# Second feed-forward block of a diffusion layer: up product as seven products of block sums, gated features kept in DRAM

## The chip, the cores and the metric

The kernel runs on one core of one Trainium2 chip. The metric is the device time of one execution in microseconds (us). The kernel before was run three times; the profile is of one further execution of it.

## What is computed

One layer over 1024 latent tokens and 256 context tokens, all float32, model width 1024, hidden width 2816. The change lies in the second SwiGLU block and in the steps around it, cut here from the reference:

```python
def layer_norm(x, g, b):
    mu = jnp.mean(xf, axis=-1, keepdims=True)
    var = jnp.mean(jnp.square(xf - mu), axis=-1, keepdims=True)
    return ((xf - mu) * lax.rsqrt(var + LN_EPS)).astype(x.dtype) * g + b

def post_norm(stream, update, g, b):
    return layer_norm(DN_ALPHA * stream + update, g, b)

def modulate(h, shift, scale):
    return h * (1 + scale) + shift

def swiglu(h, w_up, w_down):
    a, g = jnp.split(h @ w_up, 2, axis=-1)
    return (jax.nn.silu(g) * a) @ w_down

# in the layer: first SwiGLU block, then the mixer (attention and state space), then
x = post_norm(x, mod[5] * y, ln_g[layer, 1], ln_b[layer, 1])      # y: output projection of the mixer
x = post_norm(x, 0.5 * mod[8] * swiglu(modulate(x, mod[6], mod[7]), ffn2_w_up[layer], ffn2_w_down[layer]),
              ln_g[layer, 2], ln_b[layer, 2])
```

The context tokens do not reach this last part: it works on the 1024 latent tokens alone.

## The kernel before

Every large product is made of three TensorE products. An operand is split into a rounded part and the rest (`split`: ScalarE writes the rounded part, L132, VectorE the rest, L133), and `mm3` (L234) adds high by high, high by low and low by high into one PSUM bank.

**Weights** are one stream of units of 512 KB in the order of their use (`plan`). `w_dma` loads a unit into one of three buffers `ws`; `w_split` splits half a unit (128 x 512) into one of four pairs `wh`, `wl`; `take` hands out the next half units and splits up to four half units ahead. All transfers of the kernel, weights or not, are issued by one queue, SyncE's (`dq` is `nc.sync`), in the order in which the program writes them. Each engine works through its own list in that order too; a waiting instruction holds up all behind it on its engine.

**Output projection.** `token_major(8, 4, ...)` makes 512 tokens at a time: for each half of the output columns (`hf`) it goes through the eight contraction tiles and four tiles of 128 tokens. `tails=(2, 2)`: the last two contraction tiles go token tile by token tile, so that the results leave one after the other. `evac` (L1374, L1375) scales a result and adds the residual on VectorE; `norm` takes statistics by halves. Its `rest` normalises the tiles later, as a generator that `pump` moves on by a step after each unit of weights.

**Second block.** Two rounds `b` over 512 tokens each; in each, `ffn` makes two halves `h` of the hidden width. `ffn_up` makes 11 hidden tiles: `by_feature` for the linear half (one unit, 8 contraction tiles x 3 products of 128 x 512), again for the gate, then `gate` (L263 to L266: SiLU on ScalarE, product on VectorE, split of the result into `HA`, `HB`). `token_major(11, 4, ...)` follows with the down product, out of these same buffers. The up weights are loaded and split once for each `b`. The input of the second round is transposed and split by `transposed` beside the down product of the first round. The very last tiles have `TAIL = 8` contraction tiles token tile by token tile, and `out_now` (L1427, L1428) finishes and stores each at once.

## Time and profile before

| | |
|---|---|
| time of three runs | 2245.5, 2247.68, 2248.1 us (median 2247.68) |
| span of the profiled execution | 2243.0 us |
| the time outside the span, by the median | 4.7 us |
| TensorE busy in the span | 2200.6 us (98%) |
| VectorE, ScalarE, GpSimd busy | 1466.8, 735.6, 22.3 us |
| granted TensorE clock, mean | 0.998 |
| transfers | 336.67 MB, mean 150 GB/s |

The span runs from the first to the last instruction of the profiled execution; the runs' times hold the start and end of the program as well, so the sum is made on the span and carried over with the 4.7 us. Busy TensorE is not TensorE at its peak, since its matmuls overlap: what counts is the distance from one matmul's start to the next one's.

### The profile page before, as it was taken

Reading aid. Unit: us, or ns where it says so; the run is one execution under the profiler, and the core shown is the slowest. Engines: PE = TensorE matmul, PEld = TensorE weight load, DVE = VectorE, ACT = ScalarE, POOL = GpSimd, SP = SyncE. Lnnn points to the kernel's source line nnn. Section 1 sums busy time; section 2 is a strip of 40 time slices with the busy share of each in tenths; the row PEclk is TensorE's granted clock in tenths of the full one; section 3 lists DMA queues with packets and bytes.
Section 4 is the critical chain, followed back from the end, with each engine's and each line's share of the span. In section 5 each row is a group of like instructions: output and inputs, shape, how many; then the busy total and the mean of one; then the engine's idle time right before and its main releaser. Section 6 shows DMA issues by size and latency. Waiting matters only on the chain.

```text
span 2243.0 us, 32802 instructions
## 1 busy us (share of the span) xinstructions
PE 2200.6 (98%) x12536; PEld 1978.9 (88%) x12536; DVE 1466.8 (65%) x3257; ACT 735.6 (33%) x1575; POOL 22.3 (1%) x33
## 2 busy tenths in 40 slices
PE   7999999999999999999999899999999999999998
PEld 6998999889998999899899799888888888888886
DVE  7788878797888786554777467885334367334336
ACT  4322223423322223333222577433322332332331
POOL 0000000000000000000000000000000000000000
PEclk9999999999999999999999999999999999999999
DMA  9787713436433345235776763332222223322222
GB/s 348 251 294 252 264 67 114 157 125 205 133 126 123 113 133 186 84 113 193 254 262 217 189 154 95 141 131 94 97 101 94 95 93 127 108 96 102 94 94 84
DMA packets 153964, 336.67 MB, mean 150 GB/s; under 512 B 17352, under 2 KB 84936, under 8 KB 153808
## 3 DMA queue, kind: packets, MB, share of 16 engines
q1 hardware_dynamic: 153808, 334.59, 44.6%
q8 instruction: 98, 1.61, 0.3%
q14 instruction: 58, 0.48, 0.1%
HBM read 285.80 MB, written 54.70 MB: 152 GB/s over the span
## 4 chain that ended last, share of the span: by engine, by line
PE 89%; DMA 4%; DVE 3%; ACT 2%; issue 1%; SPq 1%; POOL 0%; POOLq 0%; DVEq 0%; ACTq 0%
PE pb L236 18%; PE pb L237 18%; PE pb L235 18%; PE pb L295 9%; PE pb L297 9%; PE pb L296 9%; PE pb L1251 2%; PE pb L1071 1%; PE pb L1226 1%; DMA bd<-ub 1%; PE pb L348 1%; DMA ws<-wu 1%; DVE row L231 1%; PE pb L1200 1%; ACT z L1211 1%
## 5 line engine op out<-in xcount | busy, mean ns | idle before, releaser
L235 PE MATMUL pb<-X,wh 128*128 128x384 f32 (+2 forms) x2272 | 762.9, 336 | 0.0
L237 PE MATMUL pb<-X,wl 128*128 128x384 f32 (+2 forms) x2272 | 760.6, 335 | 0.0
L133 DVE TENSOR_TENSOR wl<-ws,wh 128x512 fp32r<-128x512 f32 x596 | 395.7, 687 | 305.7 <-ACT wh L132 304.1
L132 ACT ACTIVATE wh<-ws 128x512 fp32r<-128x512 f32 x596 | 357.7, 625 | 597.3 <-PE pb L297 356.6
L236 PE MATMUL pb<-X,wh 128*128 128x512 f32 (+2 forms) x1408 | 486.2, 345 | 0.0
L235 PEld LDWEIGHTS pb<-X,wh 128*128 128x128 f32 x2272 | 429.6, 189 | 28.9
L237 PEld LDWEIGHTS pb<-X,wl 128*128 128x128 f32 x2272 | 429.3, 189 | 28.7 <-DVE wl L133 0.2
L295 PE MATMUL pb<-wh,HA 128*128 128x512 f32 x840 | 329.2, 392 | 2.2 <-DVE hid L264 1.7
L296 PE MATMUL pb<-wl,HA 128*128 128x512 f32 x840 | 326.9, 389 | 0.0
L236 PEld LDWEIGHTS pb<-X,wh 128*128 128x128 f32 x1408 | 265.7, 189 | 25.2
L236 PE MATMUL pb<-XT,wh 128*128 128x256 f32 (+2 forms) x864 | 274.4, 318 | 0.4 <-DVE XT L133 0.4
L264 DVE TENSOR_TENSOR hid<-pb,hid 128x384 f32<-128x384 f32 (+2 forms) x132 | 73.2, 555 | 237.6 <-ACT hid L263 237.4
L295 PEld LDWEIGHTS pb<-wh,HA 128*128 128x128 f32 x840 | 157.8, 188 | 35.7 <-DVE hid L264 2.6
L296 PEld LDWEIGHTS pb<-wl,HA 128*128 128x128 f32 x840 | 157.8, 188 | 31.9
L263 ACT ACTIVATE hid<-pb 128x384 f32<-128x384 f32 (+2 forms) x132 | 64.6, 489 | 359.4 <-PE pb L237 359.4
L236 PEld LDWEIGHTS pb<-XT,wh 128*128 128x128 f32 x864 | 163.8, 190 | 4.6 <-DVE XT L133 0.8
L297 PE MATMUL pb<-wh,HA 128*128 128x512 f32 x416 | 162.0, 389 | 0.0
L297 PE MATMUL pb<-wh,HB 128*128 128x512 f32 x408 | 158.8, 389 | 0.0
L265 ACT ACTIVATE HA<-hid 128x384 fp32r<-128x384 f32 (+2 forms) x132 | 69.3, 525 | 142.5 <-DVE hid L264 142.5
L297 PEld LDWEIGHTS pb<-wh,HA 128*128 128x128 f32 x416 | 78.1, 188 | 16.5
L297 PEld LDWEIGHTS pb<-wh,HB 128*128 128x128 f32 x408 | 76.6, 188 | 16.0
L1251 PE MATMUL pb<-XE,row 128*128 128x64 f32 x512 | 64.6, 272 | 0.0
(355 smaller groups left out, 2616.2 us busy)
## 6 DMA issues: line engine op xcount, KB each, us to landing
ws<-wu SPq DMA_DIRECT2D x184, 512.0 KB
ws<-wd SPq DMA_DIRECT2D x88, 512.0 KB
XE<-wada SPq DMA_DIRECT2D x36, 512.0 KB
HX<-wada SPq DMA_DIRECT2D x36, 512.0 KB
XE<-s5m SPq DMA_DIRECT2D x21, 768.0 KB
HX<-s5m SPq DMA_DIRECT2D x11, 768.0 KB
HA<-wada SPq DMA_DIRECT2D x16, 512.0 KB
ws<-wo SPq DMA_DIRECT2D x16, 512.0 KB
```

Of the source, the lines that this page charges most:

```text
L132: S.activation(h, src, AF.Copy)
L133: V.tensor_tensor(l, src, h.bitcast(F32), op=ALU.subtract)
L235: mm(p, lhsT=wh, rhs=xh, start=first, stop=False)
L236: mm(p, lhsT=wh, rhs=xl, start=False, stop=False)
L237: mm(p, lhsT=wl, rhs=xh, start=False, stop=last)
L263: S.activation(t, g, AF.Silu)
L264: V.tensor_tensor(t, a, t, op=ALU.mult)
L265: S.activation(h, t, AF.Copy)
L295: mm(b[t], lhsT=h, rhs=wh, start=f + i == 0, stop=False)
L296: mm(b[t], lhsT=h, rhs=wl, start=False, stop=False)
L297: mm(b[t], lhsT=l, rhs=wh, start=False, stop=f + i == nf - 1)
L1251: mm(o, lhsT=p, rhs=v, start=m == 0, stop=m == len(ks) - 1)
```

## The change

The second block's up product treats all 1024 tokens at once. Its weights of a hidden tile, the contraction (1024) and the tokens (1024) are each taken in two halves, the linear and the gate part of a tile as the two halves of the third side. In place of the eight products of 4 contraction tiles that this takes, seven are made, between sums of the blocks (the scheme of Strassen in Winograd's form):

- `seven(ua)` gives the seven left operands of a hidden tile: three halves of units as they are, and four sums `s1` to `s4` that VectorE makes in a tile `row` ahead of the split. The order of the products is in `ORDER`.
- `RB[1..7]` are the seven right operands, each four tiles of 128 x 512 with their two parts, made once. Those of products 1 and 2 hold the first 512 tokens (`left_part`, beside the output projection, which also writes them to DRAM as `xf`). The other five are made by `right1` to `right5`, which `ramp` calls after the second to the seventh product; they read `xf` back and transpose the second 512 tokens there.
- `product` makes one product in one bank; `add` puts the seven results together on VectorE; `gated` multiplies, splits and stores the gated tile in DRAM (`hd`, 1 MB a tile).
- The down product of all 22 hidden tiles follows, twice 512 tokens: `hid_load` reads the 22 tiles back before the first round, and `follow` those of the second round in the second half of the first.
- The normalised rows of the output projection go to DRAM (`xh2`) and come back as `z2` after the up product. The second 512 rows are normalised at once (`normed`), and the output projection's last pass has a tail of four contraction tiles. The last norm is made at once by `out_now` in both rounds.
- Five buffers for up units (three `ws`, two in `HX`), weight order and layout of the down weights adapted; the first block and the mixer run as before.

```diff
+    def seven(ua):
+        ug = ua + 1
+        h = lambda u, j: wst[u][:, j * 512:(j + 1) * 512]
+        def s1():
+            r = sums_of[ua] = rowt()
+            V.tensor_tensor(r[:, 0:512], h(ug, 0), h(ug, 1), op=ALU.add)
+            return r[:, 0:512]
...
+        return {1: ((ua,), lambda: h(ua, 0)), 2: ((ua,), lambda: h(ua, 1)), 3: ((ua,), s4), 4: ((ug,), lambda: h(ug, 1)),
+                5: ((ug,), s1), 6: ((ua,), s2), 7: ((ua, ug), s3)}
+    ORDER = [(0, 1), (0, 2), (1, 1), (1, 2), (0, 5), (1, 5), (0, 6), (1, 6), (0, 7), (1, 7), (0, 4), (0, 3), (1, 4), (1, 3)]
+    ORDER += [(f, i) for f in range(2, NF) for i in (1, 5, 6, 2, 7, 4, 3)]
...
+    def w_next(margin):
+        u = pos[0]
+        if u >= len(units) or (margin and u >= barred[0]):
+            return False
+        b = home[u][0] if u in home else turn_w[0] % NWS
+        if b in owner and last_use[owner[b]] >= pos[1] - margin:
+            assert margin, (u, b)
+            return False
+        if u in home:
+            w = home[u][1]
+        else:
+            turn_w[0] += 1
+            w = wp.tile([128, 1024], F32, name=nm("ws"), tag="ws", bufs=NWS)
+        owner[b] = u
+        nc.sync.dma_start(w, units[u])
+        wst[u] = w
+        pos[0] += 1
+        return True
...
+    def left_part(zs):
+        for k0 in (4, 6, 0, 2):
+            ks = (k0, k0 + 1)
+            bs, xs = [bank("T") for _ in ks], [half("hid") for _ in ks]
+            for k, b in zip(ks, bs):
+                for t, x in enumerate(zs):
+                    nc.tensor.transpose(b[:, t * 128:(t + 1) * 128], x[:, k * 128:(k + 1) * 128], ident)
+            V.tensor_scalar(xs[0], bs[0], gB[:, 0, k0:k0 + 1], gB[:, 1, k0:k0 + 1], op0=ALU.mult, op1=ALU.add)
+            S.activation(xs[1], bs[1], AF.Identity, scale=gB[:, 0, k0 + 1:k0 + 2], bias=gB[:, 1, k0 + 1:k0 + 2])
+            for k, x in zip(ks, xs):
...
+    def normed(t, mv, rs):
+        z = zz[4 + t]
+        V.tensor_scalar(z, z, mv[:, 0:1], rs, op0=ALU.subtract, op1=ALU.mult)
+        dq.dma_start(xh2[4 + t], z)
...
+        token_major(8, 4, src, evac, 2.2, (2, 4) if b else (2, 2), kinds="me" if b else "wm",
+                    beside=() if b else last_steps())
...
+    for i in range(2):
+        dq.dma_start(ht[:, i * 1024:(i + 1) * 1024], xf[i])
+        dq.dma_start(me[:, i * 1024:(i + 1) * 1024], xf[2 + i])
...
+    def right1(ks):
+        bs = [turned_z(k) for k in ks]
+        for k, b in zip(ks, bs):
+            V.scalar_tensor_tensor(t1f[k], b, gB[:, 0, k:k + 1], x11[k], op0=ALU.mult, op1=ALU.subtract)
+        for k in ks:
+            split(RB[5][0][k], RB[5][1][k], t1f[k])
+    def right2(ks):
+        bs, xs = [turned_z(k + 4) for k in ks], [half("hid") for k in ks]
+        for k, b, x in zip(ks, bs, xs):
+            S.activation(x, b, AF.Identity, scale=gB[:, 0, k + 4:k + 5], bias=gB[:, 1, k + 4:k + 5])
+            V.tensor_tensor(t1f[k], x, t1f[k], op=ALU.subtract)
+        for k, x in zip(ks, xs):
+            split(RB[6][0][k], RB[6][1][k], t1f[k])
+            split(RB[3][0][k], RB[3][1][k], x)
+    def right3(k):
+        V.scalar_tensor_tensor(x11[k], x11[k], gB[:, 1, k:k + 1], t1f[k], op0=ALU.add, op1=ALU.subtract)
+        split(RB[7][0][k], RB[7][1][k], x11[k])
...
+    def gated(f):
+        s = st2.pop(f)
+        zA, zB = s["A"], s["B"]
+        V.tensor_tensor(zA, zA, zB, op=ALU.mult)
+        o = hring[f % 2]
+        S.activation(o[:, 0:1024].bitcast(F32R), zA, AF.Copy)
+        yield
+        V.tensor_tensor(o[:, 1024:2048].bitcast(F32R), zA, o[:, 0:1024], op=ALU.subtract)
+        yield
+        dq.dma_start(hd[f], o)
...
+    def product(f, i):
+        settle()
+        w = take()[0]
+        s = st2.setdefault(f, {})
+        take_bank(s, i)
+        prod(s[i][0], w, RB[i])
+        if i == 1:
+            s["A"] = ztile()
+            S.activation(s["A"][:, 0:512], s[1][0], AF.Copy)
+            bfree.append(s.pop(1)[1])
+        if i == 7:
+            s["B"] = ztile()
+        A, B = s.get("A"), s.get("B")
+        lo, hi_ = slice(0, 512), slice(512, 1024)
+        if i == 6:
+            add(A[:, hi_], s, 6, A[:, lo])
+            s["u2"] = True
+        if i in (2, 6) and 2 in s and "u2" in s:
+            add(A[:, lo], s, 2, A[:, lo])
+        if i == 7:
+            add(B[:, hi_], s, 7, A[:, hi_])
+            add(A[:, hi_], s, 5, A[:, hi_], False)
+        if i == 4:
+            add(B[:, lo], s, 4, B[:, hi_])
+            add(B[:, hi_], s, 5, B[:, hi_])
+            S.activation(B, B, AF.Silu)
+        if i == 3:
+            add(A[:, hi_], s, 3, A[:, hi_])
+            later2.append(gated(f))
...
+    def ramp(n):
+        if n in (2, 3):
+            right1(range(2 * n - 4, 2 * n - 2))
+        elif n in (4, 5):
+            right2(range(2 * n - 8, 2 * n - 6))
+            if n == 5:
...
+    def hid_load(b, f):
+        if f < len(hid_room):
+            t = hid_room[f]
+            hid2[f] = t.rearrange("p (i t) -> p i t", i=2)
+            dq.dma_start(hid2[f].bitcast(F32), hd[f].rearrange("p (i t) -> p i t", i=2)[:, :, b * 512:(b + 1) * 512])
...
+    for f, i in ORDER:
+        product(f, i)
+        nprod += 1
+        ramp(nprod)
...
+    for j in range(4, NF):
+        hid_load(0, j)
+    hx = slott("HX", [128, NHX])
+    fin = [hx[:, 0:1024], hx[:, 1024:2048]]
+    z2 = [ztile() for _ in range(4)]
+    for t in range(4):
+        dq.dma_start(z2[t], xh2[t])
+    for n, i in (("g1", 2), ("b1", 3)):
+        rows[n] = rowt()
+        row_load(rows[n], i)
...
+        half_done, rest = norm(out_now)
...
+        def follow():
+            for _ in range(NF - 2):
+                yield
+            for f in range(NF):
+                if f:
+                    hid_load(1, f - 1)
+                yield
+        fol = follow()
+        token_major(NF, 4, src, evac, 2.0, (2, TAIL) if b else (2, 2), "dd", () if b else fol)
```

How the lists stand at three places. **First**, VectorE behind the output projection's second 512 tokens (`st`, `mv`, `rs` are the statistics of a tile, `XE` and `z` its rows, `wl` the rest of a weight half, `hid` the gate). Before, the normalisations (L334) of three of the four tiles:

```order
L322 BN_AGGR mv_15383<-st_15152 128x2
L324 TENSOR_SCALAR rs_15385<-mv_15383 128x1
L334 TENSOR_SCALAR XE_10579<-XE_10579,mv_15368,rs_15370 128x1024
L133 TENSOR_TENSOR wl_15390<-ws_15289,wh_15389 128x512
L133 TENSOR_TENSOR wl_15394<-ws_15289,wh_15393 128x512
L334 TENSOR_SCALAR XE_10579<-XE_10579,mv_15373,rs_15375 128x1024
L264 TENSOR_TENSOR hid_15425<-pb_15343,hid_15425 128x512
L133 TENSOR_TENSOR wl_15430<-ws_15341,wh_15429 128x512
L133 TENSOR_TENSOR wl_15434<-ws_15341,wh_15433 128x512
L334 TENSOR_SCALAR z_14781<-z_14781,mv_15378,rs_15380 128x1024
```

Now, the end of the last token tile (L1494 normalises it), then the first splits and sums of the second block (L166 is `s1`, L1550 `right1`, which reads `HB`, the block that came back from DRAM):

```order
L401 BN_STATS st_15183<-z_14806 128x6
L408 BN_AGGR mv_15382<-st_15183 128x2
L410 TENSOR_SCALAR rs_15384<-mv_15382 128x1
L1494 TENSOR_SCALAR z_14806<-z_14806,mv_15382,rs_15384 128x1024
L134 TENSOR_TENSOR wl_15401<-ws_15263,wh_15400 128x512
L134 TENSOR_TENSOR wl_15405<-ws_15263,wh_15404 128x512
L166 TENSOR_TENSOR row_15425<-HX_15206 128x512
L134 TENSOR_TENSOR wl_15424<-row_15425,wh_15423 128x512
L1550 SCALAR_TENSOR_TENSOR HB_15389<-pb_15442,gB,HB_15389 128x512
L1550 SCALAR_TENSOR_TENSOR HB_15389<-pb_15447,gB,HB_15389 128x512
L134 TENSOR_TENSOR HA_15395<-HB_15389,HA_15395 128x512 x2
L166 TENSOR_TENSOR row_15460<-ws_15265 128x512
```

The normalisations stood spread out between the next units' splits; each now stands ahead of all of these, directly behind its tile's statistics, and the making of the right operands stands between the splits.

**Second**, SyncE's queue where the down product begins. Before, from the up weights (`wu`) of a half to its down weights (`wd`):

```order
L149 DMA ws_18599<-wu 128x1024
L149 DMA ws_18638<-wu 128x1024
L149 DMA ws_18674<-wd 128x1024
L149 DMA ws_18713<-wd 128x1024
L149 DMA ws_18749<-wd 128x1024
```

Now, from the last of 18 loads of gated tiles (`hd`, 512 KB each; four more and the first three units `wd` stand further ahead, the store of the last gated tile directly ahead of the 18) to the fourth and fifth unit of down weights:

```order
L1681 DMA XT_18654<-hd_14540 128x2x512
L1708 DMA z_18675<-xh_107 128x1024
L1708 DMA z_18676<-xh_107 128x1024
L1708 DMA z_18677<-xh_107 128x1024
L1708 DMA z_18678<-xh_107 128x1024
L455 DMA row_18683<-lnr 128x1024
L455 DMA row_18685<-lnr 128x1024
L455 DMA HX_18674<-lnr 128x1024 x2
L218 DMA ws_18699<-wd 128x1024
L218 DMA ws_18737<-wd 128x1024
```

VectorE at the same place (L1595, L1599: the last gated tile; L1722, L1724: the rows `z` that came back from DRAM times and plus the rows that came with them):

```order
L1595 TENSOR_TENSOR z_18512<-z_18512,z_18592 128x1024
L1599 TENSOR_TENSOR XE_15643<-z_18512,XE_15643 128x1024
L134 TENSOR_TENSOR wl_18696<-ws_18599,wh_18695 128x512
L1722 TENSOR_TENSOR z_18675<-z_18675,row_18683 128x1024
L1724 TENSOR_TENSOR z_18675<-z_18675,row_18685 128x1024
L134 TENSOR_TENSOR wl_18716<-ws_18601,wh_18715 128x512
L1722 TENSOR_TENSOR z_18676<-z_18676,row_18683 128x1024
```

The fourth unit now stands behind 26 other transfers, and the split of the fifth half unit (`wl_18716`) behind two steps that need four of the last of them.

**Third**, VectorE between the two rounds of the down product. Before (L334, L1406, L1407: norm of the first round, beside the second round's up product):

```order
L322 BN_AGGR mv_17970<-st_17705 128x2
L324 TENSOR_SCALAR rs_17972<-mv_17970 128x1
L334 TENSOR_SCALAR XE_10579<-XE_10579,mv_17955,rs_17957 128x1024
L1406 TENSOR_TENSOR XE_10579<-XE_10579,A_2157_15327 128x1024
L1407 TENSOR_TENSOR XE_10579<-XE_10579,A_2158_15328 128x1024
L133 TENSOR_TENSOR wl_17980<-ws_17880,wh_17979 128x512
L133 TENSOR_TENSOR wl_17984<-ws_17880,wh_17983 128x512
L334 TENSOR_SCALAR HX_14046<-HX_14046,mv_17960,rs_17962 128x1024
```

Now the last of the four tiles, L1739 and L1740 its norm, then the splits of the second round's third half unit and on:

```order
L1751 TENSOR_TENSOR pb_19104<-pb_19104,row_18637 128x512
L1752 SCALAR_TENSOR_TENSOR z_18678<-z_18678,pb_19104 128x512
L401 BN_STATS st_19100<-z_18678 128x6
L408 BN_AGGR mv_19538<-st_19100 128x2
L410 TENSOR_SCALAR rs_19540<-mv_19538 128x1
L1739 SCALAR_TENSOR_TENSOR z_18678<-z_18678,mv_19538,HX_18674 128x1024
L1740 SCALAR_TENSOR_TENSOR z_18678<-z_18678,rs_19540,HX_18674 128x1024
L134 TENSOR_TENSOR wl_19554<-ws_19440,wh_19553 128x512
L134 TENSOR_TENSOR wl_19558<-ws_19440,wh_19557 128x512
```

All four tiles' chains now stand in one piece ahead of the next round's splits, of which two (the first two half units) stand ahead of the chains.

## Rows read from the trace of the kernel before

**Rows 1.** Page, part 1: busy us (share of the span) and instructions.

```profile
PE 2200.6 (98%) x12536; PEld 1978.9 (88%) x12536; DVE 1466.8 (65%) x3257; ACT 735.6 (33%) x1575; POOL 22.3 (1%) x33
```

**Rows 2.** Windows: length; busy PE, PEld, DVE, ACT, POOL; granted clock, DMA share, GB/s.

```profile
1560.00:1580.00 20.00, 20.00 (x90) 16.58 (x89) 10.36 (x15) 6.12 (x11) 0.00 (x0) 1.00 0.30 106
```

**Rows 3.** Timeline, TensorE, up product: start, us, line, instruction.

```profile
1543.44 1.03 PE L362 MATMUL pb<-ident,modl 128*128 128x128 f32 x8
...
1555.22 0.39 PE L235 MATMUL pb<-X,wh 128*128 128x512 f32 x1
...
1560.66 0.39 PE L235 MATMUL pb<-X,wh 128*128 128x512 f32 x1
```

**Rows 4.** Timeline, VectorE, output projection and up product.

```profile
1438.21 0.69 DVE L1374 TENSOR_TENSOR pb<-pb,row 128x512 f32<-128x512 f32 x1
1438.93 0.69 DVE L1375 SCALAR_TENSOR_TENSOR XE<-XE,pb 128x512 f32<-128x512 f32 x1
1439.54 0.69 DVE L1374 TENSOR_TENSOR pb<-pb,row 128x512 f32<-128x512 f32 x1
...
1448.96 1.23 DVE L1294 TENSOR_TENSOR XE<-XE,A 128x1024 f32<-128x1024 f32 x1
1450.11 0.68 DVE L133 TENSOR_TENSOR wl<-ws,wh 128x512 fp32r<-128x512 f32 x1
...
1566.93 0.69 DVE L264 TENSOR_TENSOR hid<-pb,hid 128x512 f32<-128x512 f32 x1 [2.47 <-ACT hid L263]
1568.84 1.29 DVE L133 TENSOR_TENSOR wl<-ws,wh 128x512 fp32r<-128x512 f32 x2 [1.22 <-ACT wh L132]
```

**Rows 5.** Timeline, ScalarE, the same stretch of the up product.

```profile
1567.66 0.63 ACT L265 ACTIVATE HA<-hid 128x512 fp32r<-128x512 f32 x1 [0.76 <-DVE hid L264]
1568.20 1.66 ACT L132 ACTIVATE wh<-ws 128x512 fp32r<-128x512 f32 x3
```

**Rows 6.** Groups by line and shape, ScalarE: count, busy us, mean ns, idle before.

```profile
L132 ACT ACTIVATE X<-A 128x1024 fp32r<-128x1024 f32 x4 | 4.0, 1073 | 0.0
```

**Rows 7.** Waits of the whole span: us in total, times, longest.

```profile
DVE wl L133 <- ACT wh L132: 304.1, 235, 3.3
```

**Rows 8.** Timeline, VectorE, the last four token tiles.

```profile
2217.30 0.70 DVE L508 TENSOR_TENSOR pb<-pb,row 128x512 f32<-128x512 f32 x1 [3.66 <-PE pb L297]
...
2222.74 0.70 DVE L508 TENSOR_TENSOR pb<-pb,row 128x512 f32<-128x512 f32 x1
...
2238.74 0.75 DVE L1428 SCALAR_TENSOR_TENSOR z<-z,rs,A 128x512 f32<-128x512 f32 x1
```

**Rows 9.** Timeline, GpSimd, the power of the variance for the first and last of them.

```profile
2220.03 1.46 POOL L325 TENSOR_TENSOR rs<-rs,mhalf 128x1 f32<-128x1 f32 x1 [336.87 <-DVE rs L324]
...
2236.34 0.92 POOL L325 TENSOR_TENSOR rs<-rs,mhalf 128x1 f32<-128x1 f32 x1 [3.99 <-DVE rs L324]
```

**Rows 10.** Timeline, TensorE, its last matmul.

```profile
2233.19 0.39 PE L297 MATMUL pb<-X,HB 128*128 128x512 f32 x1
```

**Rows 11.** Windows with the transfer engines full (columns as in rows 2).

```profile
28.00:32.00 4.00, 4.00 (x28) 4.00 (x28) 3.96 (x6) 2.25 (x4) 0.00 (x0) 1.00 1.02 403
...
500.00:520.00 20.00, 20.00 (x146) 19.67 (x145) 16.62 (x42) 7.03 (x15) 0.00 (x0) 1.00 1.02 347
```

**Rows 12.** Timeline, SyncE's queue: two loads of 512 KB.

```profile
2205.74 1.53 SPq L149 DMA_DIRECT2D ws<-wd  x2
```

**Rows 13.** Timeline, ScalarE, the split that waited for them.

```profile
2210.43 2.41 ACT L132 ACTIVATE X<-ws 128x512 fp32r<-128x512 f32 x4 [4.69 <-DMA ws<-wd]
```

**Rows 14.** Timeline, TensorE, where attention begins: a wait for transfers.

```profile
1265.21 0.36 PE L1200 MATMUL pb<-HB,HX 128*128 128x256 f32 x1 [2.90 <-DMA HB<-kd]
1266.78 0.45 PE L1201 MATMUL pb<-HA,HX 128*128 128x256 f32 x1 [1.22 <-DMA HA<-kd]
...
1268.31 0.63 PE L236 MATMUL pb<-X,wh 128*128 128x512 f32 x1
1268.74 0.63 PE L237 MATMUL pb<-X,wl 128*128 128x512 f32 x1
```

**Rows 15.** Windows of 2 us at that place (columns as in rows 2).

```profile
1268.00:1270.00 2.00, 2.00 (x6) 1.54 (x6) 0.03 (x1) 0.00 (x0) 0.00 (x0) 0.50 1.02 408
1270.00:1272.00 2.00, 2.00 (x10) 1.65 (x8) 1.38 (x5) 0.00 (x0) 0.00 (x0) 0.92 1.04 423
```

More of the change, by code (lines that the diff above doesn't have):

```diff
@@ L154, in w_split, with item @@
[L154 to L159 removed]
+    units, items, last_use = [], [], {}
+    wst, wsp, apart, sums_of = {}, {}, {}, {}
+    pos, ahead, out_ = [0, 0, 0], [4], [0]
+    home, owner, turn_w = {}, {}, [0]
+    barred = [10 ** 9]
+    def item(us, f):
+        for u in us:
+            last_use[u] = len(items)
+        items.append((max(us), f))
@@ new lines, in w_dma, with w_split @@
+    def w_dma(n):
+        while pos[0] < min(n, len(units)):
+            assert w_next(0)
+    ringed = set()
+    def w_split(n, must):
+        while pos[1] < min(n, len(items)):
+            i = pos[1]
+            if i not in apart and len(ringed) >= 4:
+                assert i >= must, i
+                break
+            u, f = items[i]
+            if u >= barred[0] and i >= must:
+                break
+            w_dma(u + 1)
+            if i in apart:
+                wh, wl = apart.pop(i)
@@ L170, in take @@
         pos[2] += n
-        w_split(i + max(n, ahead[0]))
-        w_dma((i + ahead[0]) // 2 + NWS - 1)
+        for j in list(ringed):
+            if j < i:
+                ringed.discard(j)
+        w_split(i + max(n, ahead[0]), i + n)
+        while w_next(2):
+            pass
         return [wsp.pop(j) for j in range(i, i + n)]
@@ L429, in hybrid_layer @@
     pos[2] = 8
-    w_split(12)
+    w_split(12, 0)
     started = ((pb8[0], pb8[1]), (pb8[2], pb8[3]))
@@ new lines, in right4, with right5, prod, settle @@
+    def right4(k):
+        V.tensor_tensor(x21[k], x21[k], t1f[k], op=ALU.subtract)
+    def right5(k):
+        split(RB[4][0][k], RB[4][1][k], x21[k])
+    st2 = {}
+    def prod(p, w, X):
+        wh, wl = w
+        for k in range(4):
+            s = slice(k * 128, (k + 1) * 128)
+            mm3(p, wh[:, s], wl[:, s], X[0][k], X[1][k], k == 0, k == 3)
+    later2 = []
+    def settle():
+        now, later2[:] = list(later2), []
+        for g in now:
+            try:
+                next(g)
+                later2.append(g)
+            except StopIteration:
+                pass
```

220 lines of the change are left out of this document (161 added, 59 removed), and 1 row of the table banks.

## The prediction

> **What bounds the kernel now.** I read the page's busy times first: TensorE is busy for 2200.6 of 2243.0 us, VectorE for 65% and ScalarE for 33% [rows 1]. Then the windows of the second block, to see whether "busy" there means "the limit": in 20 us TensorE has no gap, the clock is at full speed (the 2.4 GHz level), VectorE works half the time, the transfer engines 0.30 of it [rows 2]. The timeline gives TensorE's price: 24 matmuls of 512 columns start in 5.44 us, 0.2267 us each, and eight transposes take 1.03 [rows 3]. So in the second block a matmul removed is worth 0.2267 us at once, as long as the operands keep coming. What decides is whether VectorE, ScalarE and the queue still deliver. Their prices: VectorE starts independent steps of 512 columns 0.61 apart, dependent ones 0.72, and one of 1024 takes 1.15 [rows 4]; ScalarE takes 0.55 to 0.63 for 512 [rows 5] and 1.07 for 1024 [rows 6]. A handover costs: VectorE's product started at 1566.93, ScalarE took it up at 1567.66 and VectorE stood still for 1.22 more until 1568.84 [rows 4, 5]. Such waits of VectorE for a rounded part sum to 304.1 us in 235 places [rows 7]; today they cost nothing.
>
> **1. What is removed: -59.8 us.** A hidden tile had eight products of 4 contraction tiles with three matmuls each, 12 matmuls of 512 columns; seven remain. Over 22 tiles the up product falls from 22x8x12 = 2112 to 22x7x12 = 1848 matmuls: 264x0.2267 = 59.8 us [rows 3]. The down product and the transposes keep their counts. This is sure, and the rest asks what is lost to new waits.
>
> **2. Start of the second block: +26 us.** Let P be the end of the output projection. Its last pass now ends token tile by token tile, each 12 matmuls or 2.72 us after the one before, so the first result stands at P-8.2. Behind each, VectorE runs the scaling, statistics and normalisation in one piece. The nearest row is the end of the kernel, where such a chain, with one more pass of 1024 columns, takes 5.44 us (GpSimd's power of the variance in it) [rows 8, 9]; less 1.15 [rows 4] that is 4.3. Four chains end at P+9.0, and no weight split or right operand stands ahead of that end. TensorE has two products (P to P+5.4), then needs the transposes of those rows. The first 512 tokens come back from DRAM behind the last row store in SyncE's queue: 2 MB, about 6 us later (a load that waited for two units took 4.7 [rows 12, 13]), so at P+15.
>
> From P+9 to the third tile's last sum VectorE has 93 steps of size: 89x0.605 = 53.8, four of 1024 columns 4.6, ten dependent starts 1.2, 2.3 of waiting for the reload. Then 18 places where it makes a sum or difference, ScalarE rounds it and VectorE subtracts, with nothing between: each is exposed for 0.78 (0.1 and ScalarE's 0.63 and the way back, against the next start [rows 4, 5]): 14.0. ScalarE's own writing in `right2` and the copies of the gated tiles: 5.5. Sum 81.4, so P+90. TensorE ends its 21st product some 3 us earlier, at P+87. Unhindered, 21x2.72 and 32 transposes take 61.3 [rows 3]. The loss is 26. Its ends: all handovers covered by work in front of them, 7; every step at its busy time of 0.69 instead of its pitch, 33.
>
> **3. The other 19 hidden tiles: 0, up to +26.** TensorE needs 84x0.2267 = 19.0 us a tile. VectorE has 18 steps of 512 (10.9), two of 1024 (2.3), 0.4 for dependent ones, and exposed waits: the gated tile's copy 1.8 (1.07 and two ways), three sums 0.78 each, 1.2 behind SiLU: 5.3. That is 18.9, just below. I take 0. With 0.69 for each step it would be 20.4, 1.4 too long, 19x1.4 = 26.
>
> **4. Start of the down product: +31.5 us.** Let Q be the end of the last up product. The last gated tile needs a sum, a product, a copy and a difference, and its store is issued at Q+4.4. Behind it in SyncE's queue stand 18 loads of gated tiles, four of rows `z`, two row loads, all of 512 KB, two more, and only then the fourth unit of weights. VectorE has split four half units (four tiles of the contraction, 10.9 us of TensorE) and next in its list are L1722 and L1724, which need the first `z` and two rows, the 24th transfer at the latest. So much, with what is still under way (13.1 MB), at the 403 GB/s of a full stretch [rows 11] takes 32.4 us, and a load lands about 2.7 behind its transfer [rows 12, 13]: Q+39.7. Two passes of 1024 and the first waiting split end at Q+42.9, and TensorE, which has been idle since about Q+11.4, is at the eighth contraction tile at Q+54.3 instead of Q+22.8: 31.5. If only the weights behind it decided, 28; at the 347 GB/s of the slower full stretch [rows 11], 37.
>
> In that full stretch 403 GB/s went through [rows 11]. The Trainium skill (page "DMA: Bandwidth & Descriptors", section Specifications) puts the limit of a core's loads from device memory at about 358 GB/s; by it the 13.1 MB would take 36.6 us and the forecast would be 4 us higher. The row is above the page's limit, so it is the row that I use.
>
> **5. Between the two rounds of the down product: +13 us.** Let R be the last matmul of round one. Four chains of 5.44 [rows 8], now in one piece and from R-4.1 on, hold VectorE to R+17.7. Behind them stands the split of the third half unit, ready at R+18.4. Two half units were split ahead, 5.4 us of TensorE. It stands for 13.0. The norm stood spread out before. Bounds: 10, if the first chain starts earlier because its half is done, to 16. The stores of the four tiles also hold up SyncE's queue, but the loads behind them are needed later.
>
> **6. Clock after these stalls: +2 us.** Where attention begins TensorE waited 2.90 and 1.22 us, and afterwards its matmuls started 0.43 apart [rows 14]; the granted clock was 0.50, the 1.2 GHz level, then 0.92 [rows 15]. Ten such matmuls instead of 0.2267 cost 2.0. I count this once, at the boundary; at the two other places VectorE or the queue decides anyway.
>
> **7. The end: 0.** From the last matmul at 2233.19 [rows 10] to the end, 9.4 us, the same steps run.
>
> **Sum**: -59.8+26+0+31.5+13+2 = +12.7 on the span of 2243.0: 2255.7. The median of the runs is 4.7 above the span; so 2260.4, I say 2260.
>
> **Rivals.** *The start is covered (not slower):* if the scheduler's order lets ScalarE round one operand while VectorE makes the next, the 18 exposed places vanish, the start costs 7 and the time is 2241, faster by 0.3%. It decides once the start costs under 13. For it: products 1 and 2 of two tiles need none of the new operands. Against it: 304 us of exactly these waits in the kernel before [rows 7], and the list has the subtraction directly behind its sum. Chance 0.16. *In between:* the start at 13 to 20, or a shorter boundary (10): 2246 to 2252, within 0.2%: 0.10. *VectorE bounds the up product:* the chain of point 3 is over 19.04 a tile; at 20.4 the time is 2286. For it: my chain is 1% below; against it: VectorE's pitch of 0.61 is measured over many steps without waits. Chance 0.20. *The forecast:* 0.54. That the change does not do what it says is excluded by the lists: TensorE's has 264 rows less.
>
> **How the numbers follow.** 0.2% (4.5 us) is about what a measurement of this kernel can tell from no change. Faster: the first rival, 0.16. Same: 0.12, the in-between and the edge of the first. Slower: 0.72. The range goes from 2243 (start at about 9) to 2288 (VectorE-bound throughout, or slow transfers at both places with a partly bound up product).
>
> **What the profile of the changed kernel would show.** TensorE idle from P+5.4, with the chain of waits through L1550 and the reload `HB<-xf`, and VectorE above 90% for 80 us. Up product at TensorE 20.00 of 20 and VectorE at about 15 to 16. At the start of the down product a wait of L1722 for a transfer of about 30 us, transfer engines full, near 400 GB/s. Between the rounds TensorE waiting some 13 us for a split behind L1740. The granted clock at the lower level behind those stalls. I am wrong in step 2 if TensorE shows no gap beyond 10 us there, in step 4 if L1722 waits under 20, in step 3 if the windows of the up product show TensorE waiting for VectorE throughout.

## The result

The changed kernel takes 2273.37 us (median of four runs, 2270.1 to 2275.91), the kernel before 2246.7 us in the same comparison (2245.5 to 2248.1): the ratio is 1.0116, with a 95% interval of 1.0101 to 1.0131. It is slower by 1.2%, some 27 us. The profiled execution has a span of 2271.0 us, 28.0 more than before.

The first part of the page, to be read against [rows 1]:

```profile
PE 2165.2 (95%) x12272; PEld 1937.5 (85%) x12272; DVE 1595.5 (70%) x3421; ACT 739.7 (33%) x1547; POOL 24.6 (1%) x33
```

TensorE has 264 instructions less and is busy for 35 us less, but in a longer span: it stands more. Where it stands, the windows tell (columns as in [rows 2]: length, busy PE, PEld, DVE, ACT, POOL, granted clock, DMA share, GB/s):

```profile
1480.00:1500.00 20.00, 17.89 (x82) 13.66 (x81) 13.73 (x21) 8.70 (x15) 0.00 (x0) 0.91 0.46 172
...
1520.00:1540.00 20.00, 14.09 (x59) 11.28 (x58) 13.70 (x24) 4.87 (x8) 1.09 (x2) 0.83 0.45 170
...
1560.00:1580.00 20.00, 17.32 (x56) 11.24 (x56) 16.87 (x28) 6.59 (x11) 0.00 (x0) 0.84 0.25 82
...
1820.00:1840.00 20.00, 20.00 (x90) 16.58 (x89) 14.89 (x21) 6.58 (x10) 0.00 (x0) 1.00 0.29 106
...
1980.00:2000.00 20.00, 1.70 (x7) 0.88 (x5) 0.00 (x0) 0.00 (x0) 0.00 (x0) 0.66 1.04 385
2000.00:2020.00 20.00, 5.09 (x12) 4.03 (x13) 8.12 (x8) 1.15 (x2) 0.00 (x0) 0.50 0.94 363
...
2120.00:2140.00 20.00, 12.08 (x54) 9.67 (x52) 16.55 (x24) 3.16 (x5) 4.37 (x3) 0.92 0.30 112
2140.00:2160.00 20.00, 15.24 (x56) 12.40 (x57) 8.62 (x14) 2.42 (x4) 1.46 (x1) 0.74 0.63 227
```

From 1600 to 1960 every window reads like the one at 1820: TensorE without a gap, full clock, VectorE at 14 to 15 of 20 us. The losses are at four places around it. Their sizes come from the timeline of TensorE: the distance from each matmul's start to the next, less the 0.2267 us that it has in a full stretch [rows 3] (0.109 for a transpose), summed by place. So a slow clock counts as lost time too, which busy time hides.

| place (us in the changed kernel) | lost before | lost now | forecast |
|---|---|---|---|
| output projection, 1484 to 1512 | 0 | 5.3 | 0 |
| start of the second block, 1512 to 1605 | 0 | 28.5 | 26 |
| rest of the up product, 1605 to 1950 | 0 | 0.0 | 0 |
| start of the down product, 1950 to 2050 | 0 | 36.4 | 31.5 |
| between its two rounds, 2050 on | 0 | 15.5 | 13, and 2 for the clock |

Together 85.7; with the 59.8 of removed matmuls that is +25.9. Another 2.4 lie ahead of all this: the first transposes of the first 512 tokens, the same step in both kernels, come at 1474.45 us before and at 1476.84 now. That is scatter of single executions: in the eleven kernels of the experiments, alike up to there, the same step comes at 1473.76 to 1478.51. So spans of two profiled executions compare to some 2 us at best, and the losses by place, which start behind it, are the finer measure; I go by those.

The timeline of TensorE at these places (start, us, engine, line, instruction, idle time before and what ended it):

```profile
1493.38 0.50 PE L381 MATMUL pb<-wh,HB 128*128 128x512 f32 x1 [1.74 <-DVE XE L1508]
...
1526.61 0.33 PE L1544 MATMUL pb<-ident,z 128*128 128x128 f32 x1 [2.37 <-DVE z L1494]
...
1533.64 0.69 PE L1544 MATMUL pb<-ident,XE 128*128 128x128 f32 x2 [3.54 <-DVE HB L1550]
...
1982.34 0.47 PE L381 MATMUL pb<-wh,X 128*128 128x512 f32 x1 [1.11 <-DMA X<-hd]
2014.91 0.79 PE L382 MATMUL pb<-wl,X 128*128 128x512 f32 x1 [32.10 <-DVE wl L134]
2015.51 0.63 PE L383 MATMUL pb<-wh,X 128*128 128x512 f32 x1
2015.93 0.63 PE L381 MATMUL pb<-wh,X 128*128 128x512 f32 x1
...
2144.76 0.79 PE L382 MATMUL pb<-wl,X 128*128 128x512 f32 x1 [12.68 <-DVE wl L134]
```

And VectorE, which is named as the releaser:

```profile
1525.74 0.81 DVE L1494 TENSOR_SCALAR z<-z,mv,rs 128x1024 f32<-128x1024 f32 x1 [0.73 <-POOL rs L411]
...
1529.12 0.69 DVE L134 TENSOR_TENSOR wl<-row,wh 128x512 fp32r<-128x512 f32 x1 [0.76 <-ACT wh L133]
1532.84 1.41 DVE L1550 SCALAR_TENSOR_TENSOR HB<-pb,gB,HB 128x512 f32<-128x512 f32 x2 [3.03 <-DMA HB<-xf]
...
1970.61 0.69 DVE L134 TENSOR_TENSOR wl<-ws,wh 128x512 fp32r<-128x512 f32 x1 [2.42 <-ACT wh L133]
1971.22 0.68 DVE L1611 TENSOR_TENSOR z<-pb,z 128x512 f32<-128x512 f32 x1
...
2011.74 1.23 DVE L1722 TENSOR_TENSOR z<-z,row 128x1024 f32<-128x1024 f32 x1 [35.63 <-DMA row<-lnr]
...
2142.82 1.28 DVE L1740 SCALAR_TENSOR_TENSOR z<-z,rs,HX 128x1024 f32<-128x1024 f32 x1 [0.44 <-POOL rs L411]
2144.02 2.49 DVE L134 TENSOR_TENSOR wl<-ws,wh 128x512 fp32r<-128x512 f32 x4
```

The reader sees the three forecast waits by name: the chain of norms and the reload, then a sum of weights that waits 0.76 us for its own rounding; the residual step L1722 that stands 35.63 us for the last of the rows; the four chains that end at 2144.10 and the split behind them. After the two long waits some twelve matmuls start 0.43 apart, with the granted clock at 0.50 (the 1.2 GHz level) in the window at 2000: some 2.4 us each time. VectorE's waits for the rounded part of a weight half, such as the one of 0.76, sum up from 1515 to 1600 to 11.9 us in 13 places (waits: us in total, times, longest), and four of 0.70 in `right3` come on top:

```profile
DVE wl L134 <- ACT wh L133: 11.9, 13, 1.6
```

Eleven of the 13 stand behind a sum of weights that VectorE has just made. The two longest (1.65 and 1.64) stand behind ScalarE's SiLU and its copy of a gated tile.

### The profile page after: what moved, and what is told of

It reads as the page before. It is cut to its first block, busy times and chain, and to the rows that moved or that the text cites. A ratio compares the mean times of both kernels' runs of the same rounds, so it can differ in the third digit from the quotient of the medians.

```text
span 2271.0 us, 32457 instructions
## 1 busy us (share of the span) xinstructions
PE 2165.2 (95%) x12272; PEld 1937.5 (85%) x12272; DVE 1595.5 (70%) x3421; ACT 739.7 (33%) x1547; POOL 24.6 (1%) x33
## 4 chain that ended last, share of the span: by engine, by line
PE 81%; DVE 8%; DMA 5%; ACT 3%; issue 2%; SPq 1%; POOL 1%; POOLq 0%; ACTq 0%; DVEq 0%
PE pb L322 16%; PE pb L323 16%; PE pb L321 16%; PE pb L382 8%; PE pb L383 8%; PE pb L381 8%; PE pb L1337 2%; PE pb L1157 1%; DVE row L317 1%; PE pb L1312 1%; DVE wl L134 1%; ACT wh L133 1%; PE pb L1286 1%; PE pb L1287 1%; POOL rs L411 1%
## 5 line engine op out<-in xcount | busy, mean ns | idle before, releaser
L321 PE MATMUL pb<-X,wh 128*128 128x256 f32 (+2 forms) x1744 | 559.2, 321 | 1.1 <-ACT wh L133 1.1
L323 PE MATMUL pb<-X,wl 128*128 128x256 f32 (+2 forms) x1744 | 556.5, 319 | 0.0
L134 DVE TENSOR_TENSOR wl<-ws,wh 128x512 fp32r<-128x512 f32 x460 | 306.8, 688 | 267.2 <-ACT wh L133 264.8
L133 ACT ACTIVATE wh<-ws 128x512 fp32r<-128x512 f32 x460 | 281.1, 627 | 583.1 <-PE pb L383 362.0
L321 PEld LDWEIGHTS pb<-X,wh 128*128 128x128 f32 x1744 | 331.2, 190 | 10.3 <-ACT wh L133 2.0
L323 PEld LDWEIGHTS pb<-X,wl 128*128 128x128 f32 x1744 | 330.8, 190 | 9.3 <-DVE wl L134 0.9
L322 PE MATMUL pb<-X,wh 128*128 128x256 f32 (+2 forms) x946 | 307.5, 325 | 0.0
L322 PEld LDWEIGHTS pb<-X,wh 128*128 128x128 f32 x946 | 179.5, 190 | 7.1
L321 PE MATMUL pb<-HA,wh 128*128 128x512 f32 (+2 forms) x424 | 154.4, 364 | 3.2 <-ACT wh L133 2.2
L323 PE MATMUL pb<-HA,wl 128*128 128x512 f32 (+2 forms) x424 | 153.3, 362 | 0.0
L381 PEld LDWEIGHTS pb<-wh,HA 128*128 128x128 f32 x672 | 126.2, 188 | 29.7 <-DVE hid L350 3.0
L322 PE MATMUL pb<-HA,wh 128*128 128x512 f32 (+2 forms) x336 | 118.7, 353 | 0.0
L1611 DVE TENSOR_TENSOR z<-pb,z 128x512 f32<-128x512 f32 x154 | 105.7, 686 | 2.4 <-PE pb L323 0.7
```

The source lines that it names most:

```text
L133: S.activation(h, src, AF.Copy)
L134: V.tensor_tensor(l, src, h.bitcast(F32), op=ALU.subtract)
L321: mm(p, lhsT=wh, rhs=xh, start=first, stop=False)
L322: mm(p, lhsT=wh, rhs=xl, start=False, stop=False)
L323: mm(p, lhsT=wl, rhs=xh, start=False, stop=last)
L381: mm(b[t], lhsT=h, rhs=wh, start=f + i == 0, stop=False)
```

## Experiments

All edits are to the changed kernel unless another version is named, and the diffs are excerpts. "Lost" is always the loss of TensorE at the place, as in the table. The parts by themselves and the last version were executed once, the three whole versions four times.

**Start of the down product.** Two things wait there for the same burst: VectorE's residual steps, which stand ahead of the splits, and the fourth unit of weights, which stands behind 26 transfers. First the steps alone:

```diff
-    hi += [resid2(z2[0:4]), more()]
+    def wait_more():
+        for _ in range(11):
+            yield None
+        yield from resid2(z2[0:4])
+        yield from more()
+    hi += [wait_more()]
```

> One part alone of the start of the down product: VectorE's residual steps (rows z times and plus the norm's rows) are put 11 weight units later in its list; every transfer stays where it is. In the changed kernel TensorE stands 32.1 us there for a split that stands behind those steps. Theory (two blockers one behind the other: VectorE behind the rows, and the fourth unit of weights behind the same 26 transfers): the wait for the split goes, but the unit, which was issued at 2006.55 us in the changed kernel, still lands some 4 us later, so TensorE now stands 22 to 27 us two contraction tiles later; span about 2263 (2259 to 2267). Rival (VectorE's place in the list is the whole cause): under 5 us of idle left, span 2236 to 2241.

Span 2268.6 us; lost there 34.9 instead of 36.4. The wait moved as the theory has it, to the splits of the next unit, but it is 30.4 us, not 22 to 27. Waits of TensorE in this stretch (us in total, times, longest), the queue and ScalarE:

```profile
PE pb L381 <- ACT wh L133: 30.4, 1, 30.4
```

```profile
2007.17 21.43 SPq L218 DMA_DIRECT2D ws<-wd  x6
```

```profile
2017.50 2.41 ACT L133 ACTIVATE wh<-ws 128x512 fp32r<-128x512 f32 x4 [41.13 <-DMA ws<-wd]
```

The unit was issued at 2007.17 and could be split at 2017.50: 10.3 us, where I had allowed 4; at the 393 GB/s that this run moved from 1980 to 2012 that is the time of some 8 loads of 512 KB, so by this estimate some 8 of those ahead of it were still under way when it was issued. Now the weights alone:

```diff
+    w_dma(pos[0] + 1)
     for j in range(4, NF):
         hid_load(0, j)
```

> The other part alone: the fourth unit of down weights is issued ahead of the 18 loads of gated tiles; VectorE's list and all other transfers stay. Theory (VectorE, blocked by rows at the end of the burst, decides): TensorE still stands 32 to 35 us, span 2270 to 2274. Rival (the place of the weights is the cause): idle under 10 us, span under 2249.

Span 2273.2; lost 37.2. VectorE's step waits 37.3 us and TensorE 32.09, in the same place as in the changed kernel:

```profile
2017.75 0.80 PE L382 MATMUL pb<-wl,X 128*128 128x512 f32 x1 [32.09 <-DVE wl L134]
```

So each of the two blockers alone holds the time, and mending one gains 1.5 us or nothing. Both together:

```diff
-    for j in range(4, NF):
+    LEAD = 6
+    for j in range(4, 4 + LEAD):
         hid_load(0, j)
...
-            for _ in range(NF - 2):
+            for f in range(NF - 2):
+                if 4 + LEAD + f < NF:
+                    hid_load(0, 4 + LEAD + f)
                 yield
```

and the rows `z`, the norm's rows and the residual steps one by one in a generator between them.

> Both: six loads of gated tiles at once, the others one for each contraction tile of the first half, the rows z and the norm's rows between them, and the residual steps behind. The same bytes go. Theory (it is the order, not the bytes: a contraction tile needs 0.79 MB in 2.72 us of TensorE, 290 GB/s, under the 385 to 418 GB/s of the burst): idle under 4 us there and no low clock, 33 to 36 us gone, span 2235 to 2239. Rival (the bytes: the first half is short of transfers in any order): gaps spread over the half, 12 us or more of idle left, span 2247 or more.

Span 2241.4; lost 7.9 instead of 36.4. The same bytes go; the order was the cause. What is left is more than the 4 us forecast: the fourth unit again, behind six loads instead of 26, some 1.5 of low clock behind that wait, and 1.5 for a gated tile:

```profile
1990.91 0.51 PE L381 MATMUL pb<-wh,X 128*128 128x512 f32 x1 [4.05 <-ACT wh L133]
```

**Between the rounds.** The first round's norm goes back to single steps beside the next round:

```diff
-        half_done, rest = norm(out_now)
+        half_done, rest = norm(out_now if b else None)
...
+            def finish_row(t, z):
+                V.tensor_tensor(z, z, fin[0], op=ALU.mult)
+                V.tensor_tensor(z, z, fin[1], op=ALU.add)
+                dq.dma_start(out[t], z)
+
+            hi.append(rest(z2[0:4], finish_row))
```

> One part of the change undone at the boundary of the down product's two rounds: the first round's last norm is again made in steps beside the next round instead of at once. Theory (the four chains of 5.4 us in front of the splits are the whole 15.2 us there, 12.7 of idle and 2.2 to 2.4 of low clock): both go, span 2255 to 2257. Rival (SyncE's queue, in which the stores of the finished rows hold up three loads of gated tiles and the next units, is a second blocker): 5 us or more of idle remain, span 2261 or more.

Span 2259.0; lost 2.7 instead of 15.5. SyncE's queue is no second blocker. The rest is that a tile's three passes and a split take 3.85 us, more than the 2.72 that TensorE has for a half unit:

```profile
2144.96 0.50 PE L382 MATMUL pb<-wl,X 128*128 128x512 f32 x1 [0.82 <-DVE wl L134]
2148.81 0.50 PE L382 MATMUL pb<-wl,HA 128*128 128x512 f32 x1 [0.83 <-DVE wl L134]
```

**Start of the second block.** The reload ahead of the row stores:

```diff
-    for i in range(2):
-        dq.dma_start(ht[:, i * 1024:(i + 1) * 1024], xf[i])
-        dq.dma_start(me[:, i * 1024:(i + 1) * 1024], xf[2 + i])
...
+    def reload():
+        for _ in range(9):
+            yield
...
-                    beside=() if b else last_steps())
+                    beside=reload() if b else last_steps())
```

> At the start of the second block, the reload of the first 512 tokens (xf, 2 MB) is issued during the output projection's last pass, ahead of the four row stores behind which it stood. In the changed kernel VectorE waits 3.03 us for it and TensorE 3.54. Theory (VectorE's list is the chain there, so what it does not wait it gains): 2.5 to 3.5 us less, span 2267.5 to 2268.5. Rival (the chain of norms and the handovers decide, the reload is hidden behind them): within 1 us of 2271.

Span 2268.0; lost 25.5 instead of 28.5: what VectorE did not wait, TensorE gained. Next, the exposed handovers:

```diff
-            split(wh, wl, f())
+            src_ = f()
+            S.activation(wh, src_, AF.Copy)
...
+                settle_w()
+                pend.append((i, wl, src_, wh))
```

`settle_w` makes the subtractions that are still outstanding, those of the halves before.

> Same work in another order at the same place: of each weight half or sum ScalarE's rounding stays where it is and VectorE's subtraction stands one weight step later; of right3 the four sums stand first and the four subtractions behind. So most of the places where VectorE waits 0.69 to 0.78 us for the rounding of what it has just made (14 between 1526 and 1600 us in the changed kernel) get work in between; the number of steps on VectorE is the same. Theory (exposed handovers): 8 to 11 of the 28.6 us that TensorE loses from 1520 to 1600 go, span 2260 to 2263. Rival (VectorE's work itself is the bound, the handovers are covered elsewhere): under 3 us gained, span over 2268.

Span 2265.9; lost there 20.0 instead of 28.5, so 8.5 of the expected 8 to 11. But the span gained only 5.1, because the later subtraction did harm in the down product: 37.1 and 18.3 are lost there instead of 36.4 and 15.5, with waits of 34.55 and 15.40 instead of 32.10 and 12.68. At the start a subtraction now stands behind the chain of norms: TensorE's wait there is 5.57 where it was 2.37, while the one of 3.54 for the reload is gone:

```profile
1526.82 0.80 PE L341 MATMUL pb<-X,wl 128*128 128x512 f32 x1 [5.57 <-DVE wl L235]
...
2004.33 0.80 PE L400 MATMUL pb<-wl,X 128*128 128x512 f32 x1 [34.55 <-DVE wl L235]
...
2136.49 0.80 PE L400 MATMUL pb<-wl,X 128*128 128x512 f32 x1 [15.40 <-DVE wl L235]
```

**Output projection.** This loss was not forecast. In the changed kernel VectorE and ScalarE stand there for a store of `left_part`, which has two buffers:

```profile
1483.76 0.81 DVE L1466 TENSOR_SCALAR hid<-pb,gB 128x512 f32<-128x512 f32 x1 [2.62 <-DMA xf<-hid]
```

```profile
1484.09 0.78 ACT L1467 ACTIVATE hid<-pb,gB 128x512 f32<-128x512 f32 x1 [3.84 <-DMA xf<-hid]
```

The chain of work names the store itself (start, us, what):

```profile
1478.76 5.22 DMA xf<-hid
```

```diff
-            bs, xs = [bank("T") for _ in ks], [half("hid") for _ in ks]
+            bs = [bank("T") for _ in ks]
+            if k0 in (6, 2):
+                r = rowt()
+                xs = [r[:, 0:512], r[:, 512:1024]]
+            else:
+                xs = [half("hid") for _ in ks]
```

> In the output projection, left_part writes every second pair of tiles from a row buffer instead of the two hid buffers, so that a pair does not wait for the store of the pair before; the same stores go. In the changed kernel TensorE loses 5.1 us from 1490 to 1503, and just before VectorE and ScalarE wait 2.62 and 3.84 us for a store xf<-hid. Theory (these waits make the results late from their banks): 4 to 5 us less, span 2266 to 2267. Rival (the last pass starts on the banks of the pass before, which have to be emptied first): no change, 2270 or more.

Span 2266.4; lost there 3.0 instead of 5.3. The wait of 1.74 is gone, three of 0.30 to 0.37 for results in their banks are left, as the rival has it. So the stores account for 2.3 of the 5.3, half of what the theory expected, and the cause of the rest is not shown.

**All together**, with seven loads of gated tiles already behind the last tile's fourth product and one pass at a time in the norm:

> All together: these three, the last norm of the first round in single passes beside the second round, and at the start of the down product seven loads of gated tiles already behind the last tile's fourth product, the fourth unit of weights ahead of the others and the rows between the rest. Theory (each loss sits at a place of its own, so the gains add): from 28.0 us over the kernel before, 5 + 3 + 10 + 34 + 15 = 67 us less, span 2202 to 2208, time 2204 to 2211, ratio to the kernel before 0.981 to 0.984. Rival (one removed wait shows the next, VectorE's work in the start above all): 10 or more of them stay, time 2216 or more.

Time 2214.83 us (2212.63 to 2217.72), ratio to the kernel before 0.9852 (0.9836 to 0.9869); span 2215.9. Lost: 3.0 in the output projection, 19.6, 0, 4.3 and 1.8 at the other places. That is 57 us less than in the changed kernel, and the five parts by themselves (2.3, 3.0, 8.5, 28.5 and 12.8) make 55: the gains add. The forecast of 67 was missed because some parts bring less than was put on them; the time lies between the theory's and the rival's. Next, what the later subtraction costs was mended (against the version before):

```diff
-            if i < WO_END:
+            if not WO_END + 4 <= i < WO_END + len(ORDER):
+                settle_w()
                 V.tensor_tensor(wl, src_, wh.bitcast(F32), op=ALU.subtract)
...
-             "e": [0, 1, 2, 3], "h": [6, 7],
+             "e": [4, 0, 1, 2], "h": [6, 7],
```

> i_all with three things mended that its trace shows: the subtraction of the first four weight halves of the second block, put one step later, stood behind the four chains of norms (TensorE waited 5.59 us for it at 1526), and the same order in the down product cost 2.33 and 1.54 us; so the later subtraction is now kept to the up product from the fifth half on. And the output projection's last pass starts on the one bank that is free. Theory (these waits were made by the new order itself): 3 + 4 + 2 + 1 to 2 us less than i_all's 2215.9, span 2205 to 2208, time 2203 to 2209. Rival (they only showed what VectorE's list would cost there anyway, since it is full until 1565): under 4 us less, span 2212 or more.

Time 2209.43 us (2207.21 to 2214.54), ratio 0.9835 (0.9819 to 0.9851): 1.65% under the kernel before, and the best version that computes the layer. Span 2206.0, within its forecast; the time is 0.4 above its own. Lost: 3.0, 16.0, 0, 2.7 and 0. The free bank brought nothing: the same 3.0 stay, now as a wait of 1.59 us for ScalarE's rounding of a weight half. Its windows over the three stretches, the start of the second block, the up product and the start of the down product:

```profile
1520.00:1610.00 90.00, 81.09 (x345) 64.56 (x344) 77.96 (x119) 39.18 (x61) 0.55 (x1) 0.94 0.25 94
1610.00:1970.00 360.00, 360.00 (x1594) 298.18 (x1593) 259.49 (x369) 126.93 (x190) 0.00 (x0) 1.00 0.32 121
1970.00:2010.00 40.00, 39.28 (x167) 30.64 (x166) 16.25 (x20) 8.70 (x15) 0.00 (x0) 1.00 0.96 367
```

In the last of them 367 GB/s go with TensorE at work for 39.28 of 40 us; in the changed kernel the same transfers went with TensorE standing.

**Is VectorE's list the bound at the start?** Eight of its steps to GpSimd (against `j_all`):

```diff
-        V.tensor_tensor(x21[k], x21[k], t1f[k], op=ALU.subtract)
+        G.tensor_tensor(x21[k], x21[k], t1f[k], op=ALU.subtract)
...
-        split(RB[4][0][k], RB[4][1][k], x21[k])
+        S.activation(RB[4][0][k], x21[k], AF.Copy)
+        G.tensor_tensor(RB[4][1][k], x21[k], RB[4][0][k].bitcast(F32), op=ALU.subtract)
```

> j_all, and the eight steps of 128 x 512 that make the last right operand (right4's four differences, right5's four subtractions) are made by GpSimd, which has nothing else there, instead of VectorE. No row shows such a step on GpSimd: the only ones, of 128 x 1, took 0.92 and 1.46 us. Theory (VectorE's list bounds the start until the third tile): 8 x 0.6 = 4.8 us go from VectorE, 2 to 5 us less than j_all, as long as GpSimd takes under some 1.4 us a step (its product comes four products, 11 us, later). Rival (GpSimd is slower than that, or slows VectorE beside it): TensorE waits for the eleventh product, 0 to 10 us more than j_all.

Time 2209.61 us, ratio 0.9835 (0.9818 to 0.9851), span 2205.4: no difference to the version before. Lost at the start 16.6 against 16.0, in the output projection 4.6 against 3.0; a short stretch of low clock lies there in this execution, and at the start in `j_all`, so the two starts compare to some 2 us only. The timelines of GpSimd and VectorE show why nothing was gained:

```profile
1534.15 3.38 POOL L1603 TENSOR_TENSOR XE<-XE,HB 128x512 f32<-128x512 f32 x2 [12.14 <-PE pb L1576]
```

```profile
1534.72 1.67 DVE L134 TENSOR_TENSOR A<-HB,HA 128x512 fp32r<-128x512 f32 x1
1536.31 1.77 DVE L134 TENSOR_TENSOR HA<-hid,HA 128x512 fp32r<-128x512 f32 x1
1538.01 0.68 DVE L134 TENSOR_TENSOR A<-HB,HA 128x512 fp32r<-128x512 f32 x1
```

Beside the eight steps on GpSimd seven of VectorE's take 1.32 to 1.78 us instead of 0.68: 6.9 us more, against the 4.8 that it was relieved of. To tell whether the steps cost nothing on VectorE or their gain was lost again, they were left out. The wait of `j_all` to watch is this one:

```profile
1557.66 0.50 PE L342 MATMUL pb<-A,wl 128*128 128x512 f32 x1 [2.13 <-DVE wl L235]
```

> j_all with the eight steps that k_gpsimd gave to GpSimd left out altogether: right4's four differences and right5's four subtractions (the last right operand then holds other values; the same matmuls run). k_gpsimd gained nothing (span 2205.4 against 2206.0). Theory (the steps do cost VectorE's list there, and on GpSimd their gain was lost again because VectorE's own steps beside GpSimd took 1.66 to 1.78 us instead of 0.69): without them the wait of TensorE of 2.13 us at 1557 goes, and of the 16 us that TensorE loses in j_all from 1520 to 1600 2 to 4 go. Rival (VectorE's list is not what TensorE waits for there): within 1 us of 16.

Span 2199.9; lost at the start 12.0 instead of 16.0, and the wait at 1557 is gone. So 8 steps, 4.8 us, are worth 4.0: VectorE's list is still the bound in that part of the best version, and on GpSimd their gain was lost again.

## Why the prediction came out as it did

The sign and the mechanisms were right; the time was 13 us low (2260 against 2273.4). On the span it is 2255.7 against 2271.0; outside the span lie 2.4 us now, where I had carried over 4.7. That 4.7 was itself an error: it set a median against the span of another, quicker execution. Where time and span of one execution are on record, 1.8 to 2.3 lie between them (2272.88 and 2271.0; the kernel before, 2249.18 and 2247.4). With 1.9 I would have said 2257.6, so by luck it made the forecast look 3 us better. The 15.3 on the span are 5.3 of the output projection, 4.9, 2.5 and 0.5 at the other three places, and the 2.4 ahead of them (15.6; the kernel before loses 0.3 at the same places).

1. **Removed matmuls, -59.8**: right. The up product runs without a gap from 1605 to 1950, at the pitch of [rows 3], and the places' losses with this gain make up the measured difference.
2. **Start of the second block, 26**: 28.5. The parts were right: with P at 1518.3 the last row was normalised by 1526.55, P+8.3 where I had P+9, and the reload's first part was there 5.74 us after its issue at 1526.99 (chain of work), P+14.4 where I had P+15. The chain of a token tile took 4.03 (L1494 at 1521.71 and 1525.74), not 4.3, in part since the normalisation by two numbers a row passes 1024 columns in 0.73, where I took 1.15 from a step with two full operands [rows 4]. The handovers are shown by f_late_rest (8.5 of the 14.0 that I had put on them, by an order that covers part of them), the reload by e_reload (3.0; I had 2.3), VectorE's list by l_less. Low clock (0.83 and 0.84 in two of the windows) I had not counted here: some 26 matmuls and transposes that waited for nothing start at the slow pitch and take 6 us of the 28.5. What the place would lose at full clock is not settled, since TensorE might then wait longer for VectorE.
3. **Rest of the up product, 0**: right. VectorE is busy 14 to 15 of 20 us; the rival of a VectorE-bound up product is out.
4. **Start of the down product, 31.5**: 36.4. The mechanism is the one forecast: L1722 waited until 2011.74. The last up product's last matmul started at 1969.07, so with Q at 1969.3 that is Q+42.4, not Q+39.7. Of these 2.7 us 1.9 lie ahead of the burst: the store of the last gated tile was issued at 1975.55 (chain of work), Q+6.3 and not Q+4.4, because the split of a weight half stood ahead of the tile's sum and waited 2.42 for its rounding. The burst itself took 0.9 longer (391 GB/s from 1980 to 2012, where I took 403 [rows 11]). TensorE stood for 33.6 there, 2.1 more than forecast, of which 1.3 was a wait for a gated tile, `X<-hd`, that no term had. The other 2.8 is the clock, which I had left out there on the ground that VectorE decides. It does not: from 2014.91 on TensorE has no wait any more and still starts a matmul every 0.43. In j_all, without the long wait, the stretch has a clock of 1.00. The remark that weights alone would cost 28 was right in kind (a wait of 30.4 in a_resid_late).
5. **Between the rounds, 13**, and 6. **clock, 2**: 12.8 of idle and 2.6 behind it, and d_norm_late takes 12.8 of them away. Right to half a microsecond.
7. **The end, 0**: 9.8 us from the last matmul to the end in both.
8. **What failed**: the output projection. I had found nothing there to price and so put it at zero; it costs 5.3. The two buffers of `left_part` are read by stores to DRAM now, where they were free after a subtraction before, and a store holds its buffer for 5.22 us (from 1478.76 in the chain of work; ScalarE starts on the buffer at 1484.09, VectorE on the other at 1483.76). h_left_rows shows 2.3 of the 5.3 for these stores; the cause of the rest stays open. SyncE's list named these stores, and [rows 13] had a price near theirs. With two buffers and a pair of tiles every 3.6 us (transposes at 1476.84 and 1480.46) it could not be hidden.

The Trainium skill (page "DMA: Bandwidth & Descriptors", section Specifications) gave 358 GB/s and a forecast 4 us higher. The burst ran at 391 GB/s from 1980 to 2012, above it: the row was the better guide, though it was itself a little high, and that the time came out nearer to the page's sum is owed to the late store, the clock and the output projection.

Of the rivals none happened. "The start is covered" needed the 18 handovers hidden by the order as it stands; up to 1600 us 15 were exposed, eleven behind sums of weights and four in `right3`, for 11.4 us or 0.76 each, where I had 0.78.

Two of the signs that I had named did not come, and both were chosen against my own sum. VectorE is not above 90% for 80 us: it is busy for 64.3 of 85 us from 1515 to 1600, and the sum of step 2 itself holds 21.8 of waits in 81.4. And TensorE has no gap beyond 10 us there, which was to prove step 2 wrong: its longest waits are 3.54 and 2.37. The loss is there all the same, as 19 waits of 15.4 us together and what the slow pitch and the restarts behind them cost.

Not settled: what of the last 3.0 us in the output projection is the banks and what ScalarE's list; and which part of the 16.0 at the start in the best version is the chain of norms (a wait of 2.37 stands there in the changed kernel and in the best version) and which VectorE's list, beyond the 4.0 that l_less shows.

## What to carry to other kernels

A stage that saves TensorE work moves the limit to the seams: here 59.8 us were gained in a full stretch, and 85.7 lost where operands are first made and stored, where a burst of loads begins and where a norm stands in one piece. Read the list of each engine at the seams for what stands ahead of the next operand, and look for two blockers behind one another: here a fix of one alone brought 1.5 us or nothing, both together 28.5. And put a thing that is waited for soon (a weight unit) ahead of things that are only needed later (18 tiles of 22), even where the bytes are the same.

## What the runs showed of the hardware

- **GpSimd beside VectorE.** A step of 128 x 512 with two operands in SBUF takes 1.7 us on GpSimd (3.38 for two) while VectorE works beside it; no run shows it alone. VectorE's steps with both operands in SBUF that run wholly beside it take 1.66 to 1.78 instead of 0.68. A step that reads one operand from PSUM does not (the group of L1647 in the same kernel, two in 1.40):

```profile
1557.14 1.40 DVE L1647 TENSOR_TENSOR z<-pb,z 128x512 f32<-128x512 f32 x2
1558.46 1.72 DVE L235 TENSOR_TENSOR wl<-HX,wh 128x512 fp32r<-128x512 f32 x1
1560.10 1.78 DVE L181 TENSOR_TENSOR row<-HX,row 128x512 f32<-128x512 f32 x1
```

  The Trainium skill (page "SBUF — State Buffer", section Who interferes with whom) says just this: a VectorE instruction with two inputs in SBUF contends with a GpSimd instruction that reads SBUF, one with at most one such input, outside its two-port modes, does not. The rows agree, and give the price.
- **A load's way in a full stretch.** 10.3 us from issue to use at the end of a burst at 393 GB/s (a_resid_late), against 4.7 for the pair of [rows 13].
- **The clock.** After 32.1 us and after 12.68 us of idle alike, TensorE started some 12 matmuls 0.43 apart (granted clock 0.50, the 1.2 GHz level, in the window at 2000), which cost 2.3 to 2.4 us. Two idle stretches of 1.74 and 0.37 us in the output projection were followed by the like: seven matmuls 0.43 to 0.59 apart from 1494.71 on, with a granted clock of 0.61 from 1494 to 1498.
